# Two transformer blocks on one core: modulation transposes emitted later, four plain column blocks ahead of the quarter products

## The chip, the core and the metric

The kernel runs on one core of a Trainium2 chip. The metric is the device time of one execution in microseconds (us), lower is better. TensorE (PE) does the matrix products; its weight loads (PEld) overlap them. ScalarE (ACT), VectorE (DVE) and GpSimd (POOL) do the elementwise work, and SyncE's queue (SP) issues every DMA. An engine works through its own queue in order.

## The reference

`reference()` computes two blocks in float32 on a sequence of 1024 tokens with 1024 features. What matters here is the swiglu layer, which the first block holds twice, and the modulation that comes from a conditioning vector:

```python
def swiglu(h, w_gu, w_down):
    g, u = jnp.split(h @ w_gu, 2, axis=-1)        # w_gu: 1024 x 5632
    return (jax.nn.silu(g) * u) @ w_down          # w_down: 2816 x 1024

mod = (cs @ w_ada[l] + b_ada[l]).reshape(B, N_MOD, D)      # first block, 9 x 1024
mod = c @ w_ada[l] + b_ada[l]                              # second block, 3 x 1024, for l = 0, 1
x = x + HALF_STEP * gt1 * swiglu(h, w_gu1[l], w_down1[l])  # FFN 1; then the mixer; then FFN 2
```

## The kernel before

**Precision.** Every float32 matrix is split into a high and a low part. `split` (line 262 onwards) makes the high part with a copy on ACT (line 255) and the low part with a subtraction on DVE (line 277). One product of a 128x128 weight block with a 128x512 half of the tokens is then three matmuls: high by high, high by low, low by high (lines 328 to 330, or 601 to 603).

**The FFN.** `ffn` (line 629) runs twice, as FFN 1 (0 to 740 us of the trace) and FFN 2 (1480 to 2060 us). The 2816 columns are 22 blocks of 128, each with a gate half and an up half. The first `n` = 3 blocks are plain: `gu_start` or `gu` multiplies gate and up for one half of the tokens, 8 x 3 matmuls each, so a block takes 2 x 2 x 24 = 96 matmuls. Their weights go through the queue `ws` (class `Weights`): `get(i, ahead)` splits view i at once if that has not happened yet, and fetches and splits further views only as far as `ahead` says. The other 19 blocks go through `products` (line 558), a seven-product scheme on quarters: 7 products of 4 x 3 matmuls, 84 per block. For it `combine` (line 517) forms sums of token quarters (`hs`, `ht`, `T`) on DVE, POOL and ACT, beside the plain blocks of the second token half. For each product the weight quarters `a11` to `s4` are made by POOL sums (`ws` tiles, line 574) and split by ACT and DVE into a `W` pair; `prep` does that LAG = 4 products ahead. The two raw tiles of a block are loaded by `fetch`. Finished activations are split (`act`) and stored to DRAM by `spill`. Then the down stage (`out`) multiplies by `w_down`.

**Modulation chunks.** `ada` (line 436) makes 512 columns of a modulation vector as filler beside the products: four loads (`adaw`), eight multiply-adds on DVE into `adacc` (lines 454 and 456), then four PE transposes (line 469) and a DVE sum along the row (line 471). For the gate rows of the second block a product with ones (line 488) takes the place of the transposes. `fill()` starts a chunk: `beside(n)` calls it ahead of product n when n % 14 is 3 and n is under 105, and the down stage calls it twice per group from its second group on while chunks are left (14 chunks in FFN 1, 12 in FFN 2).

**Order.** The code emits work through `Pipe`: `go` starts a generator and steps it and all live ones, and `products` steps them once after each product. The framework's planner then makes each engine's queue out of that order: it may let a ready instruction pass one that still waits. Tiles of one tag share a fixed number of slots: 43 of 4 KB per partition (tag "u": weights, splits, `H`, `T`, `W`, `act`, loads), 14 of 2 KB (tag "hf": `ws`, `pc`, `pq`, `e`, `adacc`) and 8 PSUM banks (`ps`).

```python
pipe.until(lambda: (id(H), "combined") in self.ready)      # end of the plain blocks
...
fetch(0)                                                   # products: raw weights of its first two blocks
fetch(1)
for n in range(-1, self.LAG):
    prep(n)                                                # first sums and splits
```

Of the kernel before, what the change touches and what calls it, by code (L numbers as in the profile page):

```python
# [18 lines left out]
P = 128  # L19
T = 1024  # L20
HT = 512
NK = 8
DFF = 2816
NFF = DFF // P
# [26 lines left out]
class Pipe:  # L51
# [25 lines left out]
    def beside(self):  # L77
        for f in self.side:
            f.feed(self)
# [81 lines left out]
class Weights:  # L161
# [7 lines left out]
    def fetch(self, n):  # L169
        while len(self.stg) < min(n, len(self.views)):  # L170
            self.stg.append(self.load(*self.views[len(self.stg)]))
# [21 lines left out]
class Build:  # L193
# [239 lines left out]
                self.nc.vector.tensor_tensor(p[:, 1], t, p[:, 0].bitcast(F32), OP.subtract)  # L433
            yield

    def ada(self, w, c, bias, out, c0, row=None, ahead=False):


        nc = self.nc
        def load(q):  # L440
            t = self.U(F32, (P, 2, 512), "adaw")
            self.load(t, w[c0 // HT][:, 2 * q:2 * q + 2])
            return t

        if ahead:
            ts = [load(q) for q in range(4)]
            yield
        acc = self.half(name="adacc")
        for q in range(4):
            t = ts[q] if ahead else load(q)  # L450
            for j in range(2):
                k = 2 * q + j
                if k == 0:
                    nc.vector.tensor_scalar(acc, t[:, j], c[:, k:k + 1], None, OP.mult)
                else:
                    nc.vector.scalar_tensor_tensor(acc, t[:, j], c[:, k:k + 1], acc, OP.mult, OP.add)
            if not ahead:
                yield
        if row is not None:
            b = self.half(name="brow")  # L460
            self.load(b[0:1], row[1])
            ps = self.total(acc)
            yield
            nc.vector.scalar_tensor_tensor(b[0:1], ps[0:1], 1.0, b[0:1], OP.add, OP.add)
            self.store(row[0], b[0:1])
            return
        ps = self.ps([P, 4, P])
        for j in range(4):
            nc.tensor.transpose(ps[:, j], acc[:, j * P:(j + 1) * P], self.ident)
        f = c0 // P  # L470
        nc.vector.tensor_reduce(out[:, f:f + 4], ps, AX.X, OP.add)
        nc.vector.tensor_tensor(out[:, f:f + 4], out[:, f:f + 4], bias[:, f:f + 4], OP.add)
# [76 lines left out]
            2: ("s3", "a11", "a21", OP.subtract), 3: ("s4", "a12", "s2", OP.subtract)}  # L549
    LAG = 4  # L550

    def products(self, pairs, view, B, post, beside):

        nc, pipe = self.nc, self.pipe
        mm = nc.tensor.matmul
        seq = [(i, j) for i in range(len(pairs)) for j in range(7)]
        raw, W, Wr = {}, {}, {}

        def fetch(i):
            if i < len(pairs):
                r = [self.fetch_w(*view(pairs[i], o)) for o in range(2)]
                for o in range(2):
                    for q in range(2):
                        Wr[i, f"a{o + 1}{q + 1}"] = r[o].rearrange("p k c -> p (k c)")[:, HALVES[q]]

        def sums(n):

            for d, (name, a, b, op) in self.SUMS.items():  # L570
                if (n - d) % 7 == 0 and 0 <= (n - d) // 7 < len(pairs):
                    i = (n - d) // 7
                    Wr[i, name] = t = self.half(name="ws")
                    nc.gpsimd.tensor_tensor(t, Wr[i, a], Wr[i, b], op)

        def prep(n):
            sums(n)
            if 0 <= n < len(seq):
                i, j = seq[n]
                W[n] = p = self.pair("W")  # L580
                self.split(Wr[i, self.SEVEN[j][0]], p[:, 0], p[:, 1])
                if j == 2:
                    fetch(i + 2)

        fetch(0)
        fetch(1)
        for n in range(-1, self.LAG):
            prep(n)
        for n, (i, j) in enumerate(seq):
            beside(n)  # L590
            prep(n + self.LAG)
            if j == 0:
                acc = {s: self.ps() for s in "xyz"}
                g = post(pairs[i])
                next(g)
                started, held = set(), {}
            w, b, s = W.pop(n), B[self.SEVEN[j][1]], self.SEVEN[j][2]
            o = acc[s]
            for k in range(4):
                wh, wl = (w[:, q, k * P:(k + 1) * P] for q in range(2))  # L600
                mm(o, wh, b[k][:, 0], start=k == 0 and s not in started, stop=False, skip_group_check=True)  # L601
                mm(o, wh, b[k][:, 1], start=False, stop=False, skip_group_check=True)  # L602
                mm(o, wl, b[k][:, 0], start=False, stop=k == 3, skip_group_check=True)  # L603
            started.add(s)
            if j in (0, 2, 3):
                c = self.half(name="pc")
                self.copy(c, o)
                held[j] = c
            elif j == 6:
                g.send(o)  # L610
                pipe.start(g)
            else:
                c = self.half(name="pq")
                nc.vector.tensor_tensor(c, o, held[{1: 0, 4: 3, 5: 2}[j]], OP.add)  # L614
                g.send(c)
            pipe.step()
            pipe.beside()

    def ffn(self, H, X, XD, wgu, wdown, gate, fill, done, late, squares=True, begin=False):
# [2 lines left out]

        nc, pipe = self.nc, self.pipe

        n, kept = 3, range(18, NFF)
        groups = [[18, 19, 20]] + [list(range(f, f + 3)) for f in range(0, 15, 3)] + [[15, 16, 17, 21]]
        G = len(groups)
        act, order, views = {}, {}, []
# [13 lines left out]
        def gu(f, h, ahead=2, parts=1):  # L642
            pg, pu = self.ps(), self.ps()
            yield from self.gemm(pg, ws.get(order[f, 0], ahead), 0, H, h, parts)
            if parts > 1:
                yield
            yield from self.gemm(pu, ws.get(order[f, 1], ahead), 0, H, h, parts)
            yield
            yield from swiglu(f, h, pg, pu)
# [9 lines left out]
        def swiglu(f, h, pg, pu):  # L659
            e = self.half(name="e")  # L660
            self.act(e, pg, AF.Silu)
            nc.vector.tensor_tensor(e, e, pu, OP.mult)
            yield
            spill(f, h, e)

        def gu_start(f):
            w, p = [ws.get(order[f, o], 2 if f == o == 0 else 1) for o in range(2)], [self.ps(), self.ps()]
            for ks in range(4), range(4, NK):
                for o in range(2):
                    yield from self.gemm(p[o], w[o], 0, H, 0, 1, ks)  # L670
                yield
            yield from swiglu(f, 0, *p)
# [37 lines left out]
            ws.begin(2)  # L710
        yield
        if begin:
            items = [gu_start(f) for f in range(n)]
            for g in items:
                next(g)
            yield
            for g in items:
                pipe.go(g)
        else:
            pipe.until(self.whole(H, 0))  # L720
            for f in range(n):
                pipe.go(gu(f, 0, 2 if f == 0 else 0, 2), 4)
        pipe.until(self.whole(H, 1))
        B = {}
        sums = self.combine(H, B)
        for f in range(n):
            pipe.go(gu(f, 1, 1 if f == n - 1 else 0, 4), 8)
            if f == 0:
                pipe.start(sums)
        pipe.until(lambda: (id(H), "combined") in self.ready)  # L730
        rest = list(range(n, NFF))

        def beside(i):
            if i % 14 == 3 and i < 105:
                fill()
            if i == 7 * len(rest) - 4:
                wd.fetch(1)
            if i == 7 * len(rest) - 1:
                wd.split(1)

        self.products(rest, lambda f, o: (wgu[o * NFF + f], NK, P), B, post, beside)
        def load_x(k):
            if k < NK:
                X[k] = self.U(name="x")
# [1180 lines left out]
    def run(self):  # L1925
        nc, a, pipe = self.nc, self.a, self.pipe
        self.consts()
        cs = self.small([P, 8], name="cs")
        self.sigmoid(cs, self.v("c"))
        nc.vector.tensor_tensor(cs, cs, self.v("c"), OP.mult)  # L1930
        mod, mod2, coef = self.mod, self.mod2, self.coef
        wa = a["w_ada"]

        def ada1(c0):
            return self.ada(wa, cs, self.v("b_ada"), mod, c0, ahead=c0 < 2048)

        def ada2(l, c0):
            row = (self.g1[l][:, c0 - 2048:c0 - 1536], a["b_ada_2"][l:l + 1, c0:c0 + 512]) if c0 >= 2048 else None
            return self.ada(a["w_ada_2"][l], self.v("c_2"), self.v("b_ada_2")[:, 24 * l:24 * l + 24],
                            mod2[:, 24 * l:24 * l + 24], c0, row)  # L1940

        def scale_col(i, sc, g, ks=slice(0, 8)):
            out = coef[:, i:i + 8]
# [5 lines left out]
        H = self.new_h()  # L1949
# [71 lines left out]
        prep, rest = self.mlstm_prep(heads), Stream(second(), self.R1)  # L2021
# [29 lines left out]
        out = self.w_out(Y, YD, a["w_out"], mod[:, 40:48], X, XD, to_ffn, lambda: next(ffn))  # L2051
# [133 lines left out]
```

## Time and profile before

| | us |
|---|---|
| median of 3 runs | 3318.3 (3317.18 to 3319.18) |
| the profiled execution | 3313.98 |
| its span, first to last instruction | 3312.2 |
| PE busy in it | 3180.8 (96%) |
| DVE, ACT, POOL busy | 2218.0, 1413.6, 486.8 |

The profiled execution is 4.3 us faster than the median. Busy time of PE counts overlapping matmuls once. "Idle before" is what an engine waited ahead of an instruction, and the releaser is the work whose end let it go. The granted clock of PE is 1.00 at 2.4 GHz and 0.50 at 1.2 GHz.

### The profile page before, as it was taken

How to read it: one execution, taken by the hardware profiler on the slowest of the kernel's cores; microseconds unless marked ns; L12 is line 12 of the kernel's file. 1: busy time of each engine (PE TensorE's matmuls, PEld its weight loads, DVE VectorE, ACT ScalarE, POOL GpSimd, SP SyncE). 2: the span in 40 equal slices, each digit the busy share in tenths (PEclk: the TensorE clock that was granted, in tenths of full speed). 3: DMA queues.
4: the chain of work that ended last, by engine and by line, in shares of the span. 5: the costliest groups of instructions: out<-in, count | busy, mean ns of one | idle time of the engine just before them, and what ended most of it. 6: DMA issues, size and time to landing. Idle time of an engine off the chain costs nothing.

```text
span 3312.2 us, 38901 instructions
## 1 busy us (share of the span) xinstructions
PE 3180.8 (96%) x14420; PEld 2594.4 (78%) x14420; DVE 2218.0 (67%) x3349; ACT 1413.6 (43%) x2399; POOL 486.8 (15%) x328
## 2 busy tenths in 40 slices
PE   8799999999999979998999999999999999999998
PEld 5677788887877768886777888878888777888777
DVE  6866666746378877668666657464756886665787
ACT  4343341113466654553333421054346834444770
POOL 0533220000122243415223200000000000000000
PEclk9899999999999979999999999999999999999999
DMA  6344428714554466463444275233422333432233
GB/s 258 127 153 153 153 82 295 252 70 124 150 147 121 113 172 187 119 217 114 153 153 153 102 252 210 85 108 108 121 77 71 108 121 116 145 94 65 71 134 108
DMA packets 177261, 460.38 MB, mean 139 GB/s; under 512 B 17944, under 2 KB 20888, under 8 KB 177072
## 3 DMA queue, kind: packets, MB, share of 16 engines
q1 hardware_dynamic: 177072, 457.91, 41.9%
q8 instruction: 113, 1.85, 0.2%
q14 instruction: 76, 0.62, 0.1%
HBM read 340.19 MB, written 117.65 MB: 138 GB/s over the span
## 4 chain that ended last, share of the span: by engine, by line
PE 46%; DVE 5%; ACT 2%; issue 2%; DMA 2%; POOL 0%; SPq 0%; DVEq 0%; ACTq 0%; POOLq 0%
PE ps L328 8%; PE ps L330 8%; PE ps L329 8%; PE ps L601 2%; PE ps L603 2%; PE ps L602 2%; PE ps L1806 2%; PE ps L1882 2%; PE ps L1883 1%; PE ps L1599 1%; PE ps L1867 1%; PE ps L1600 1%; PE ps L1601 1%; PE ps L1881 1%; PE ps L1868 1%
## 5 line engine op out<-in xcount | busy, mean ns | idle before, releaser
L328 PE MATMUL ps<-H,wh 128*128 128x512 f32 x1296 | 515.7, 398 | 16.6 <-ACT wh L255 12.5
L330 PE MATMUL ps<-H,wl 128*128 128x512 f32 x1296 | 510.2, 394 | 1.9 <-DVE wl L277 1.9
L329 PE MATMUL ps<-H,wh 128*128 128x512 f32 x1296 | 508.5, 393 | 0.0
L328 PEld LDWEIGHTS ps<-H,wh 128*128 128x128 f32 x1296 | 245.9, 190 | 72.4 <-ACT wh L255 14.2
L330 PEld LDWEIGHTS ps<-H,wl 128*128 128x128 f32 x1296 | 245.7, 190 | 56.7 <-DVE wl L277 3.9
L329 PEld LDWEIGHTS ps<-H,wh 128*128 128x128 f32 x1296 | 246.2, 190 | 51.1 <-issue 1.7
L255 ACT ACTIVATE wh<-stg 128x1024 fp32r<-128x1024 f32 (+1 forms) x157 | 154.0, 990 | 308.8 <-PE ps L329 96.4
L703 DVE SCALAR_TENSOR_TENSOR x<-ps,coef,x 128x512 f32<-128x512 f32 x224 | 167.7, 750 | 165.5 <-PE ps L330 164.6
L328 PE MATMUL ps<-act,wh 128*128 128x512 f32 x704 | 276.2, 392 | 0.0
L330 PE MATMUL ps<-act,wl 128*128 128x512 f32 x704 | 274.1, 389 | 0.0
L329 PE MATMUL ps<-act,wh 128*128 128x512 f32 x704 | 273.9, 389 | 0.0
L277 DVE TENSOR_TENSOR wl<-stg,wh 128x1024 fp32r<-128x1024 f32 (+1 forms) x173 | 210.0, 1220 | 75.7 <-ACT wh L255 68.7
L601 PE MATMUL ps<-T,W 128*128 128x512 f32 x608 | 237.6, 391 | 5.5 <-DVE pq L614 4.8
L602 PE MATMUL ps<-T,W 128*128 128x512 f32 x608 | 237.3, 390 | 0.0
L603 PE MATMUL ps<-T,W 128*128 128x512 f32 x608 | 237.1, 390 | 0.0
L1809 DVE TENSOR_REDUCE bmc<-ps 128x1 f32<-128x512 f32 x256 | 164.7, 684 | 49.9 <-PE ps L1806 49.8
L601 PE MATMUL ps<-H,W 128*128 128x512 f32 x456 | 182.6, 400 | 10.7 <-ACT W L255 10.7
L250 ACT ACTIVATE bE<-ps 128x512 f32<-128x512 f32 x256 | 138.3, 590 | 102.9 <-PE ps L1868 72.6
L603 PE MATMUL ps<-H,W 128*128 128x512 f32 x456 | 179.8, 394 | 1.4 <-DVE W L277 1.4
L602 PE MATMUL ps<-H,W 128*128 128x512 f32 x456 | 179.8, 394 | 0.0
L281 DVE TENSOR_TENSOR bEl<-bE,bEh 128x1024 fp32r<-128x1024 f32 x128 | 155.3, 1218 | 33.5 <-ACT bEh L255 17.8
L614 DVE TENSOR_TENSOR pq<-ps,pc 128x512 f32<-128x512 f32 x114 | 78.5, 688 | 137.8 <-PE ps L603 137.6
(364 smaller groups left out, 7038.4 us busy)
## 6 DMA issues: line engine op xcount, KB each, us to landing
act<-act SPq DMA_DIRECT2D x144, 512.0 KB
adaw<-in_w_ada SPq DMA_DIRECT2D x120, 512.0 KB
stg<-in_w_gu SPq DMA_DIRECT2D x88, 512.0 KB
stg<-in_w_in SPq DMA_DIRECT2D x69, 512.0 KB
stg<-in_w_down SPq DMA_DIRECT2D x56, 384.0 KB
stg<-in_w_out SPq DMA_DIRECT2D x28, 512.0 KB
y<-y SPq DMA_DIRECT2D x22, 512.0 KB
x<-xspill SPq DMA_DIRECT2D x16, 512.0 KB
```

Of the source, the lines that this page charges most:

```text
L250: i = self.nc.scalar.activation(out, in_, func, **kw)
L255: self.nc.scalar.activation(out, in_, AF.Copy, scale=scale)
L277: self.nc.vector.tensor_tensor(lo, src, hi.bitcast(F32), OP.subtract)
L281: eng.tensor_tensor(lo, e, hi.bitcast(F32), OP.subtract)
L328: mm(ps, wh, rh, start=k == 0, stop=False)
L329: mm(ps, wh, rl, start=False, stop=False)
L330: mm(ps, wl, rh, start=False, stop=k == n - 1)
L601: mm(o, wh, b[k][:, 0], start=k == 0 and s not in started, stop=False, skip_group_check=True)
L602: mm(o, wh, b[k][:, 1], start=False, stop=False, skip_group_check=True)
L603: mm(o, wl, b[k][:, 0], start=False, stop=k == 3, skip_group_check=True)
L703: nc.vector.scalar_tensor_tensor(x, ps, gate[:, m:m + 1], x, OP.mult, OP.add)
L1809: nc.vector.tensor_reduce(mc[:, 8 * h + i:8 * h + i + 1], pss[h], AX.X, OP.max)
```

## The change

Four things. `ada` gets a number `late` (2 for every chunk that runs as filler): it lets two steps pass between the last multiply-add and the transposes (or the product with ones), and for the transposes two more between them and the DVE sum. `fill()` comes ahead of products with n % 14 = 8 in place of 3, which makes 7 chunks under 105 in place of 8; the remaining one moves to the down stage. The number of plain blocks `n` rises from 3 to 4, so 18 blocks are left for the products. The first half of the tokens still takes only the first three blocks at the place where it did; the fourth block runs for both halves in `ready()`, which `products` calls after its first loads, the first POOL sums and the splits of its products 0 and 1, and before the loads of its second block and the splits of products 2 and 3. The third block's `gu` call for the second half has `ahead` 0 in place of 1.

```diff
@@ -433,7 +433,7 @@
                 self.nc.vector.tensor_tensor(p[:, 1], t, p[:, 0].bitcast(F32), OP.subtract)
             yield
 
-    def ada(self, w, c, bias, out, c0, row=None, ahead=False):
+    def ada(self, w, c, bias, out, c0, row=None, ahead=False, late=0):
 
 
         nc = self.nc
@@ -459,14 +459,20 @@
         if row is not None:
             b = self.half(name="brow")
             self.load(b[0:1], row[1])
+            for _ in range(late):
+                yield
             ps = self.total(acc)
             yield
             nc.vector.scalar_tensor_tensor(b[0:1], ps[0:1], 1.0, b[0:1], OP.add, OP.add)
             self.store(row[0], b[0:1])
             return
+        for _ in range(late):
+            yield
         ps = self.ps([P, 4, P])
         for j in range(4):
             nc.tensor.transpose(ps[:, j], acc[:, j * P:(j + 1) * P], self.ident)
+        for _ in range(late):
+            yield
         f = c0 // P
         nc.vector.tensor_reduce(out[:, f:f + 4], ps, AX.X, OP.add)
         nc.vector.tensor_tensor(out[:, f:f + 4], out[:, f:f + 4], bias[:, f:f + 4], OP.add)
@@ -549,7 +555,7 @@
             2: ("s3", "a11", "a21", OP.subtract), 3: ("s4", "a12", "s2", OP.subtract)}
     LAG = 4
 
-    def products(self, pairs, view, B, post, beside):
+    def products(self, pairs, view, B, post, beside, ready):
 
 
 
@@ -583,8 +589,10 @@
                     fetch(i + 2)
 
         fetch(0)
-        fetch(1)
         for n in range(-1, self.LAG):
+            if n == 2:
+                ready()
+                fetch(1)
             prep(n)
         for n, (i, j) in enumerate(seq):
             beside(n)
@@ -622,7 +630,7 @@
 
         nc, pipe = self.nc, self.pipe
 
-        n, kept = 3, range(18, NFF)
+        n, kept = 4, range(18, NFF)
         groups = [[18, 19, 20]] + [list(range(f, f + 3)) for f in range(0, 15, 3)] + [[15, 16, 17, 21]]
         G = len(groups)
         act, order, views = {}, {}, []
@@ -710,7 +718,7 @@
             ws.begin(2)
         yield
         if begin:
-            items = [gu_start(f) for f in range(n)]
+            items = [gu_start(f) for f in range(n - 1)]
             for g in items:
                 next(g)
             yield
@@ -718,27 +726,32 @@
                 pipe.go(g)
         else:
             pipe.until(self.whole(H, 0))
-            for f in range(n):
+            for f in range(n - 1):
                 pipe.go(gu(f, 0, 2 if f == 0 else 0, 2), 4)
         pipe.until(self.whole(H, 1))
         B = {}
         sums = self.combine(H, B)
-        for f in range(n):
-            pipe.go(gu(f, 1, 1 if f == n - 1 else 0, 4), 8)
+        for f in range(n - 1):
+            pipe.go(gu(f, 1, 0, 4), 8)
             if f == 0:
                 pipe.start(sums)
-        pipe.until(lambda: (id(H), "combined") in self.ready)
+
+        def ready():
+            for h in range(2):
+                pipe.go(gu(n - 1, h, 0, 4), 8)
+            pipe.until(lambda: (id(H), "combined") in self.ready)
+
         rest = list(range(n, NFF))
 
         def beside(i):
-            if i % 14 == 3 and i < 105:
+            if i % 14 == 8 and i < 105:
                 fill()
             if i == 7 * len(rest) - 4:
                 wd.fetch(1)
             if i == 7 * len(rest) - 1:
                 wd.split(1)
 
-        self.products(rest, lambda f, o: (wgu[o * NFF + f], NK, P), B, post, beside)
+        self.products(rest, lambda f, o: (wgu[o * NFF + f], NK, P), B, post, beside, ready)
         def load_x(k):
             if k < NK:
                 X[k] = self.U(name="x")
@@ -1932,12 +1945,12 @@
         wa = a["w_ada"]
 
         def ada1(c0):
-            return self.ada(wa, cs, self.v("b_ada"), mod, c0, ahead=c0 < 2048)
+            return self.ada(wa, cs, self.v("b_ada"), mod, c0, ahead=c0 < 2048, late=2 * (c0 >= 2048))
 
         def ada2(l, c0):
             row = (self.g1[l][:, c0 - 2048:c0 - 1536], a["b_ada_2"][l:l + 1, c0:c0 + 512]) if c0 >= 2048 else None
             return self.ada(a["w_ada_2"][l], self.v("c_2"), self.v("b_ada_2")[:, 24 * l:24 * l + 24],
-                            mod2[:, 24 * l:24 * l + 24], c0, row)
+                            mod2[:, 24 * l:24 * l + 24], c0, row, late=2)
 
         def scale_col(i, sc, g, ks=slice(0, 8)):
             out = coef[:, i:i + 8]
```

## Rows read from the trace of the kernel before

**Rows 1.** The page's part 1: busy us (share of the span), instructions.
```profile
PE 3180.8 (96%) x14420; PEld 2594.4 (78%) x14420; DVE 2218.0 (67%) x3349; ACT 1413.6 (43%) x2399; POOL 486.8 (15%) x328
```

**Rows 2.** Waits of PE in FFN 1: us in total, times, longest.
```profile
PE ps L469 <- DVE adacc L456: 13.9, 8, 5.4
PE ps L601 <- ACT W L255: 8.9, 1, 8.9
...
PE ps L601 <- DVE pq L614: 1.6, 1, 1.6
```

**Rows 3.** The same of FFN 2.
```profile
PE ps L469 <- DVE adacc L456: 11.2, 6, 3.8
PE ps L601 <- DVE pq L614: 3.1, 1, 3.1
PE ps L488 <- DVE adacc L456: 2.8, 2, 1.5
PE ps L601 <- ACT W L255: 1.8, 1, 1.8
```

**Rows 4.** Timeline of PE, FFN 1: start, us, line, tiles, form, idle before, releaser.
```profile
113.66 0.39 PE L330 MATMUL ps<-H,wl 128*128 128x512 f32 x1
122.95 0.80 PE L601 MATMUL ps<-H,W 128*128 128x512 f32 x1 [8.90 <-ACT W L255]
...
131.54 0.40 PE L601 MATMUL ps<-H,W 128*128 128x512 f32 x1
131.77 0.39 PE L602 MATMUL ps<-H,W 128*128 128x512 f32 x1
...
153.97 1.11 PE L469 MATMUL ps<-ident,adacc 128*128 128x128 f32 x4 [5.37 <-DVE adacc L456]
...
158.59 0.39 PE L601 MATMUL ps<-H,W 128*128 128x512 f32 x1
```

**Rows 5.** One stretch: us, then PE, PEld, DVE, ACT, POOL busy, PEclk, DMA share, GB/s.
```profile
126.00:128.00 2.00, 2.00 (x6) 1.55 (x5) 0.00 (x0) 0.06 (x1) 1.92 (x3) 0.50 1.02 414
```

**Rows 6.** Timeline of PE, FFN 2.
```profile
1545.17 0.50 PE L601 MATMUL ps<-H,W 128*128 128x512 f32 x1 [1.83 <-ACT W L255]
...
1575.57 1.11 PE L469 MATMUL ps<-ident,adacc 128*128 128x128 f32 x4 [3.77 <-DVE adacc L456]
...
1578.50 0.40 PE L603 MATMUL ps<-H,W 128*128 128x512 f32 x1
```

**Rows 7.** Timelines of SP, ACT, DVE and POOL ahead of FFN 1's products.
```profile
117.75 3.73 SPq L285 DMA_DIRECT2D stg<-in_w_gu  x6
...
122.27 1.15 ACT L255 ACTIVATE W<-stg 128x512 fp32r<-128x512 f32 x2 [1.54 <-DMA stg<-in_w_gu]
...
117.19 7.03 DVE L277 TENSOR_TENSOR T<-ht,T 128x512 fp32r<-128x512 f32 x8
124.15 1.28 DVE L277 TENSOR_TENSOR W<-stg,W 128x512 fp32r<-128x512 f32 x2
...
124.27 2.29 POOL L574 TENSOR_TENSOR ws<-stg 128x512 f32<-128x512 f32 x1 [4.21 <-DMA stg<-in_w_gu]
```

**Rows 8.** The same of FFN 2: SP, POOL.
```profile
1539.37 4.75 SPq L285 DMA_DIRECT2D stg<-in_w_gu  x6
...
1546.69 1.55 POOL L574 TENSOR_TENSOR ws<-stg 128x512 f32<-128x512 f32 x1 [4.96 <-DMA stg<-in_w_gu]
```

**Rows 9.** Timelines of ACT and DVE: a plain block's weight split.
```profile
1497.16 1.05 ACT L255 ACTIVATE wh<-stg 128x1024 fp32r<-128x1024 f32 x1
...
1500.44 1.22 DVE L277 TENSOR_TENSOR wl<-stg,wh 128x1024 fp32r<-128x1024 f32 x1
```

**Rows 10.** Timeline of PE: the second token half of x comes in.
```profile
53.46 1.03 PE L392 MATMUL ps<-ident,xin 128*128 128x128 f32 x8
```

**Rows 11.** Two stretches (columns as in group 5): FFN 1's down stage, the mixer.
```profile
560.00:740.00 180.00, 180.00 (x804) 148.71 (x803) 115.74 (x166) 23.18 (x29) 0.00 (x0) 1.00 0.50 172
740.00:1480.00 740.00, 698.05 (x3378) 577.66 (x3377) 519.34 (x920) 401.48 (x714) 186.76 (x124) 0.97 0.51 150
```

## The prediction

> **What bounds the kernel now.** I read the page's first part before anything else: PE is busy for 3180.8 of 3312.2 us [rows 1], so time can only be won where PE waits or runs slowly, and every matmul added is paid in full. Next come the waits of PE, taken for each FFN by itself, since the change touches nothing else by hand. In FFN 1 PE waits 13.9 us ahead of the modulation transposes for the last multiply-add (eight waits, the longest 5.4), 8.9 us once for the first split of a quarter weight, and 1.6 us for a DVE sum [rows 2]. In FFN 2 the same places cost 11.2 us (six waits, the longest 3.8), 2.8 us where a product with ones takes the transposes' place, 1.8 and 3.1 us [rows 3]. The timeline of PE shows where the big ones stand: 8.90 us between the last plain matmul and the first product, and 5.37 us ahead of the first transposes [rows 4]; 1.83 and 3.77 us in FFN 2 [rows 6].
>
> The timeline shows a second loss behind the long waits. At full speed one matmul starts 0.23 us after the other (131.54 to 131.77). From 122.95 to 131.54 there are 18 of them in 8.59 us, where 18 x 0.23 = 4.1 would do [rows 4]; the granted clock in that stretch is 0.50, the 1.2 GHz level [rows 5]. So 4.4 us are lost there (a wait of 0.7 for the low part is in it). From 153.97 to 158.59 there are nine matmuls and four transposes of a quarter of the columns, ten matmul times or 2.3 us, in 4.62 us: 2.3 lost [rows 4]. In FFN 2, five matmuls and four transposes take 1575.57 to 1578.50, 2.93 us for six times 0.23: 1.6 lost [rows 6]. The short waits of 1.2 to 1.5 us I count without such a loss.
>
> **Transposes two products later.** A chunk's last multiply-add comes out at most 5.4 us after PE has reached its transposes [rows 2, 4], usually about 8.5 / 7 = 1.2. Two products are 24 matmuls of 0.23, 5.5 us, so every one of these waits is covered: by PE's own products, whose splits are made four ahead. The number of transposes does not change. The DVE sum of a row then waits for transposes that ended two products before, so nothing queued behind it on DVE is held. Removed: 13.9 - 5.4 = 8.5 us in FFN 1, 11.2 - 3.8 = 7.4 and 2.8 in FFN 2, together 18.7 us; the two first waits (5.4 and 3.8) are counted with the starts below. If the cover were gone the price would be these same waits. `adacc` keeps its hf slot and `ps` its bank longer; by the code at most eight of the 14 hf tiles are in use around a chunk, so I take nothing for it.
>
> **Fill at product 8 and one chunk moved.** The first chunk no longer falls among the late first splits. The eighth goes to the down stage, where PE has no idle at all beside six such chunks (180.00 of 180.00 us, DVE at 115.74) [rows 11]: nothing, bounded by one wait of 1.2 us per FFN.
>
> **The fourth plain block.** It replaces 84 matmuls by 96 in each FFN: 24 x 0.23 = 5.5 us added for certain.
>
> **What the starts lose now and then.** Removed in FFN 1: 8.9 + 4.4 + 1.6 (a DVE sum stuck behind the chunk's multiply-adds) + 5.4 + 2.3 = 22.6 us [rows 2, 4]. In FFN 2: 1.8 + 3.1 + 3.8 + 1.6 = 10.3 us [rows 3, 6]. The 22 us that the fourth block gives PE to do (96 x 0.23) run beside the sums of token quarters, the first POOL sums and the first four splits.
>
> But the fourth block needs weights, and here the change adds waits. Views 6 and 7 are its gate and up weights. In FFN 1 they are loaded with the early ones, and view 6 is split early too. View 7 is split only when `gu` gets to its up half, behind the splits of products 0 and 1 and the third block's activation. PE ends the third block at 114.05 and has the gate half, 24 x 0.23 = 5.5 us, so it wants view 7 at 119.6. ACT is held until 122.27, since SP issues the quarter weights' loads only at 117.75, behind an activation store [rows 7]. Two W splits (1.15), an activation split (half of that) and the high part (1.05) [rows 7, 9] put view 7 at 125.0: PE waits 5.5. DVE ends those W parts at 124.15 + 1.28, then 0.6 and 1.22 for the low part [rows 7, 9]: 127.3, where the third matmul could have begun at 125.5: 1.8 more. After a wait of 5.4 us the clock cost 2.3, so 9.6 us in all. Queued behind that matmul on PE are the block's second token half and all products.
>
> In FFN 2 neither view is prefetched: with `ahead` 0 view 6 is loaded when it is to be split. Its load stands third on SP, behind the two that start at 1539.37; the second of them lets POOL go at 1546.69 [rows 8]. One load lands 2.0 us after the other in FFN 1 (122.27 and 124.27, rows of ACT and POOL) [rows 7], so view 6 is there at 1548.7 and its high part at 1549.7. PE ended the third block at 1545.17 - 1.83 = 1543.3 [rows 6]: it waits 6.4, for the low part 0.8 more, and 2.3 for the clock: 9.5 us. View 7's load is next on SP and its split is ready well within the gate half. Together 19.1 us of new losses. The lower bound is none, if the planner gets these splits ahead of the others. The upper bound is that the starts lose the 32.9 us of before.
>
> The Trainium skill has a rule against this place. "SBUF — State Buffer", section "Who interferes with whom", says that a VectorE instruction with two SBUF inputs competes with a GpSimd instruction that reads SBUF, and that one of them blocks until the other is through. The trace agrees as far as it goes: eight T subtractions beside POOL take 7.03 us, 0.88 each, two W ones 1.28, 0.64 each [rows 7]. By that rule the low parts of views 6 and 7 could each wait for one more POOL sum; at the 1.55 us of rows 8 the sum below would be 3.1 us higher, 3294.3.
>
> The loads of the products' second block now follow the fourth block and its stores on SP. They are wanted at product 3, behind the second token half (48 x 0.23 = 11 us) and three products (8 us), and take about 5 us to land (117.75 to 122.27) [rows 7]: nothing. In FFN 1's first token half two more loads (1 MB, 2.5 us at the 414 GB/s of rows 5) and one split come ahead of the second half of x. Its transposes follow PE's other work without a wait [rows 10], so I take nothing; without that cover it would be up to 2.5 us.
>
> **Sum.** Removed 22.6 + 10.3 + 18.7 = 51.6; added 5.5 + 19.1 = 24.6; net 27.0 us less. The profiled execution (3313.98 us, span 3312.2) would come to 3287.0. It lies 4.3 us under the median of 3318.3, from which the forecast is made: 3291.3 us.
>
> **Rivals.** *No new waits.* The splits of views 6 and 7 come in time; then only the matmuls are added: 51.6 - 5.5 = 46.1 less, 3272.2 us. For it speaks that view 7's raw tile is long there in FFN 1, against it the order of the tiles and SP's late issue. *The starts gain nothing.* Beside the fourth block the 43 slots of tag u are nearly full (16 H, 16 T, four weight parts, two raw tiles, two W, one or two activations by the code), so the next raw tiles and W pairs wait for PE to free some, and what the starts lost comes back as other waits. Then 18.7 - 5.5 = 13.2 less, 3305.1 us. *The change doesn't do what it says.* The planner orders the queues by its own model; if it places the transposes right behind their sums again, 13.9 + 11.2 + 2.8 us of waits and the 3.9 us of slow clock stay: 27.0 - 31.8, or 4.8 us more, 3323.1. Against it: PE follows the code's order closely in this trace, and the transposes are now written two products later. *Slower.* The planner sorts the queues of the later stages anew, since its clock has shifted. The place is the mixer, where PE idles 740.00 - 698.05 = 42 us [rows 11]. If its waits doubled, the sum would be 42 - 27 = 15 us more, 3333.3; it decides from 27 us of added idle on. Nothing in the code of that stage changes, so it is unlikely.
>
> **How the numbers follow.** The forecast (3280 to 3300 by the bounds of the new waits) gets 0.55, no new waits 0.14, starts without gain 0.17, the unmoved transposes 0.08, the mixer 0.06. The range reaches from a little below the first rival to a little above the second: 3268 to 3308, with 0.86 inside. A measurement can tell about 0.2%, 6.6 us, from no change. Faster by more: the first three, 0.86; within: 0.08; slower: 0.06.
>
> **What would show it.** In the changed kernel's waits of PE, the rows "L469 <- adacc" and "L488 <- adacc" should be gone. Ahead of the products no wait for W should stand, and PE should wait 5 to 7 us inside the fourth block, for wh of view 7 in FFN 1 and for the load and wh of view 6 in FFN 2, followed by a stretch at clock 0.50. Matmuls of lines 328 to 330 should be 64 more per line and those of 601 to 603 56 fewer. The down stages should still show no idle. I am wrong if waits for adacc remain, if products stop for W or pq after the fourth block, or if idle outside the FFNs changes by more than a few us.

## The result and the profile after

| | before | after |
|---|---|---|
| median, us | 3317.7 (4 runs) | 3287.2 (4 runs) |
| ratio to before, 95% interval | | 0.9909 [0.9892, 0.9926] |
| span of the profiled execution, us | 3312.2 | 3285.2 |

The change makes the kernel 0.9% faster, 30.5 us by the medians. The forecast was 3291.3 us with a range of 3268 to 3308. In the profiled executions the span is 27.0 us shorter. Times are medians of fast executions; one of the four of e4_fill3 took 15802.6 us at a granted clock of 0.186 and is left out.

The page's first part after the change (rows 1 before): PE's busy time falls by 3.2 us although 24 matmuls were added, and its idle time from 131.4 to 107.6 us. A matmul at the slow clock counts as busy for longer, so what is won in slow stretches stands in the busy time.

```profile
PE 3177.6 (97%) x14444; PEld 2596.1 (79%) x14444; DVE 2214.4 (67%) x3333; ACT 1406.1 (43%) x2383; POOL 460.5 (14%) x320
```

The waits of PE up to 740 us, FFN 1 (rows 2 before; us in total, times, longest). `wh` and `wl` are the high and low part of a plain block's weights. No line for adacc is left, and none for W. Of the 14.6 us for wh, 10.4 are new; the other 4.2 us stood at the first matmul of the kernel before too.

```profile
PE ps L328 <- ACT wh L255: 14.6, 2, 10.4
...
PE ps L330 <- DVE wl L277: 1.4, 2, 0.7
...
PE ps L609 <- DVE pq L622: 0.8, 2, 0.6
```

The same for FFN 2, 1480 to 2060 us (rows 3 before; FFN 2 now begins at 1459.00, and PE waits nowhere between there and 1480). Here too everything about adacc has gone, and 4.0 us for wh and 4.0 us for wl stand in its place.

```profile
PE ps L330 <- DVE wl L277: 5.0, 2, 4.0
PE ps L328 <- ACT wh L255: 4.6, 2, 4.0
PE ps L609 <- DVE pq L622: 0.6, 2, 0.3
```

The timeline of PE in FFN 1 (rows 4 before). The fourth block starts behind the third without a gap; after its gate half PE stops for 10.41 us. From 130.94 to 139.16 there are 17 matmuls in 8.22 us, at a granted clock of 0.50 from 131 to 138; at 0.23 each they would take 3.9.

```profile
120.14 0.39 PE L330 MATMUL ps<-H,wl 128*128 128x512 f32 x1
130.94 0.79 PE L328 MATMUL ps<-H,wh 128*128 128x512 f32 x1 [10.41 <-ACT wh L255]
...
132.78 0.79 PE L330 MATMUL ps<-H,wl 128*128 128x512 f32 x1 [0.61 <-DVE wl L277]
...
139.16 0.40 PE L330 MATMUL ps<-H,wl 128*128 128x512 f32 x1
```

In FFN 2 (rows 6 before) PE stops ahead of the first matmul of the fourth block and again two matmuls later. Between 1537 and 1541 the granted clock is 0.50; at 1541.92 PE is back at full pace.

```profile
1531.51 0.77 PE L328 MATMUL ps<-H,wh 128*128 128x512 f32 x1 [4.03 <-ACT wh L255]
1532.07 0.63 PE L329 MATMUL ps<-H,wh 128*128 128x512 f32 x1
1536.71 0.79 PE L330 MATMUL ps<-H,wl 128*128 128x512 f32 x1 [4.01 <-DVE wl L277]
...
1541.92 0.40 PE L330 MATMUL ps<-H,wl 128*128 128x512 f32 x1
```

Where the 27 us went is read from the first matmul of three stages: FFN 1's down stage, FFN 2's first plain block, FFN 2's down stage. Before:

```profile
512.64 0.39 PE L328 MATMUL ps<-act,wh 128*128 128x512 f32 x1
...
1474.91 0.39 PE L328 MATMUL ps<-H,wh 128*128 128x512 f32 x1
...
1936.15 0.39 PE L328 MATMUL ps<-act,wh 128*128 128x512 f32 x1
```

After:

```profile
499.18 0.39 PE L328 MATMUL ps<-act,wh 128*128 128x512 f32 x1
...
1459.00 0.39 PE L328 MATMUL ps<-H,wh 128*128 128x512 f32 x1
...
1908.54 0.39 PE L328 MATMUL ps<-act,wh 128*128 128x512 f32 x1
```

FFN 1 up to its down stage is 13.5 us shorter (512.64 to 499.18). FFN 2 up to its down stage took 461.2 us and takes 449.5, 11.7 less. What lies between, with the mixer, went from 962.3 to 959.8, and the rest from 1376.1 to 1376.7.

### The profile page after: what moved, and what is told of

It is laid out like the page before. It is cut to its first block, busy times and chain, and to the rows that moved or that the text cites. A ratio compares the mean times of both kernels' runs of the same rounds, so it can differ in the third digit from the quotient of the medians.

```text
span 3285.2 us, 38924 instructions
## 1 busy us (share of the span) xinstructions
PE 3177.6 (97%) x14444; PEld 2596.1 (79%) x14444; DVE 2214.4 (67%) x3333; ACT 1406.1 (43%) x2383; POOL 460.5 (14%) x320
## 4 chain that ended last, share of the span: by engine, by line
PE 50%; DVE 3%; ACT 2%; issue 1%; DMA 1%; DVEq 0%; ACTq 0%
PE ps L328 8%; PE ps L330 8%; PE ps L329 8%; PE ps L609 3%; PE ps L611 3%; PE ps L610 3%; PE ps L1613 2%; PE ps L1612 2%; PE ps L1614 2%; PE ps L1819 2%; PE ps L1895 1%; PE ps L1896 1%; PE ps L1894 1%; PE ps L1880 1%; PE ps L1881 1%
## 5 line engine op out<-in xcount | busy, mean ns | idle before, releaser
L328 PE MATMUL ps<-H,wh 128*128 128x512 f32 x1360 | 542.9, 400 | 30.9 <-ACT wh L255 27.1
L330 PE MATMUL ps<-H,wl 128*128 128x512 f32 x1360 | 536.9, 395 | 6.8 <-DVE wl L277 6.7
L329 PE MATMUL ps<-H,wh 128*128 128x512 f32 x1360 | 534.9, 393 | 0.0
L328 PEld LDWEIGHTS ps<-H,wh 128*128 128x128 f32 x1360 | 259.1, 191 | 90.4 <-ACT wh L255 29.6
L330 PEld LDWEIGHTS ps<-H,wl 128*128 128x128 f32 x1360 | 258.4, 190 | 66.2 <-DVE wl L277 10.6
L329 PEld LDWEIGHTS ps<-H,wh 128*128 128x128 f32 x1360 | 259.3, 191 | 53.8 <-issue 1.7
L609 PE MATMUL ps<-T,W 128*128 128x512 f32 x576 | 224.6, 390 | 1.4 <-DVE pq L622 1.4
L611 PE MATMUL ps<-T,W 128*128 128x512 f32 x576 | 224.2, 389 | 0.0
L610 PE MATMUL ps<-T,W 128*128 128x512 f32 x576 | 224.1, 389 | 0.0
L609 PE MATMUL ps<-H,W 128*128 128x512 f32 x432 | 170.1, 394 | 0.0
L611 PE MATMUL ps<-H,W 128*128 128x512 f32 x432 | 168.2, 389 | 0.0
L610 PE MATMUL ps<-H,W 128*128 128x512 f32 x432 | 168.1, 389 | 0.0
```

The source lines that it names most:

```text
L328: mm(ps, wh, rh, start=k == 0, stop=False)
L329: mm(ps, wh, rl, start=False, stop=False)
L330: mm(ps, wl, rh, start=False, stop=k == n - 1)
```

## The experiments

Nine kernels. Every ratio is to runs of the kernel before on the same chip; the medians of the kernel before lay between 3314.7 and 3317.7 us. The columns FFN 1 and FFN 2 are the two stretches just described, in the profiled execution (512.6 and 461.2 before).

| kernel | us | ratio, 95% interval | FFN 1 | FFN 2 |
|---|---|---|---|---|
| changed kernel | 3287.2 | 0.9909 [0.9892, 0.9926] | 499.2 | 449.5 |
| e1_late_only | 3280.4 | 0.9899 [0.9886, 0.9911] | 497.3 | 445.6 |
| e2_no_late | 3303.1 | 0.9968 [0.9956, 0.9980] | 503.9 | 457.1 |
| e3_early_views | 3261.3 | 0.9841 [0.9828, 0.9853] | 483.6 | 437.9 |
| e4_fill3 | 3283.7 | 0.9907 [0.9892, 0.9921] | 495.4 | 448.0 |
| e5_late_fill8 | 3272.8 | 0.9866 [0.9851, 0.9881] | 491.9 | 440.0 |
| e6_fetch_only | 3285.5 | 0.9908 [0.9894, 0.9923] | 496.3 | 449.7 |
| e7_views_late1 | 3275.7 | 0.9873 [0.9856, 0.9889] | 488.7 | 443.7 |
| e8_half_deferred | 3282.5 | 0.9897 [0.9882, 0.9912] | 492.7 | 442.9 |
| e9_ready_first | 3279.8 | 0.9900 [0.9884, 0.9917] | 493.6 | 446.2 |

### e1_late_only: the delays alone

The edit, to the kernel before (the row form and the two calls get `late` as in the change); fill, `n` and `products` stay as they are there.

```diff
-    def ada(self, w, c, bias, out, c0, row=None, ahead=False):
+    def ada(self, w, c, bias, out, c0, row=None, ahead=False, late=0):
...
+        for _ in range(late):
+            yield
         ps = self.ps([P, 4, P])
         for j in range(4):
             nc.tensor.transpose(ps[:, j], acc[:, j * P:(j + 1) * P], self.ident)
+        for _ in range(late):
+            yield
```

> The kernel before with the two delays of `late` alone: chunks still start at n % 14 = 3, three plain blocks, first splits where they were. Theory A (the forecast's terms add up, the block is worth what its sum says): the steady waits of 8.5 + 7.4 + 2.8 us go, and the two first waits (5.4, 3.8) with 3.9 us of slow clock too, since the transposes come 5.5 us later and the last multiply-add was at most 5.4 late: 31.8 us less, about 3286 us, and the start of the products still shows 8.9 us (FFN 1) and 1.8 us (FFN 2) of waits for W. By this the rest of the change is worth about nothing. Theory B (the late multiply-adds are a lack of VectorE throughput, so the wait only moves to another DVE product): the waits for adacc go but waits for pq or W of 1 us a chunk take their place, 0 to 9 us less, 3309 to 3318 us.

Measured: 3280.4 us, 0.9899. That is as fast as the whole change (the intervals overlap) and somewhat faster than theory A's 3286. The waits of PE in FFN 1 show no adacc, while the old wait ahead of the products stands as before:

```profile
PE ps L607 <- ACT W L255: 8.8, 1, 8.8
...
PE ps L607 <- DVE pq L620: 2.1, 1, 2.1
PE ps L609 <- DVE W L277: 1.9, 1, 1.9
```

FFN 1 is 15.3 us shorter than before and FFN 2 15.7. Theory B falls: no wait takes the place of the 14 steady ones. What followed from the forecast's own terms also holds: the rest of the change, as placed, brings nothing on top of the delays.

### e2_no_late: the change without the delays

```diff
-            return self.ada(wa, cs, self.v("b_ada"), mod, c0, ahead=c0 < 2048, late=2 * (c0 >= 2048))
+            return self.ada(wa, cs, self.v("b_ada"), mod, c0, ahead=c0 < 2048, late=0)
...
-                            mod2[:, 24 * l:24 * l + 24], c0, row, late=2)
+                            mod2[:, 24 * l:24 * l + 24], c0, row, late=0)
```

> The changed kernel with late = 0: fourth plain block, early splits and fill at n % 14 = 8 stay. Theory A: about 14 waits for adacc of 1.2 to 1.5 us are back, 18.7 us, none of them over 2 us since the first chunk is clear of the late splits: 3305 to 3307 us. Theory B (block and fill carry the gain, the delays none): within 4 us of the changed kernel's 3287.

Measured: 3303.1 us, 0.9968. The waits of PE in FFN 1, and below them those of FFN 2:

```profile
PE ps L473 <- DVE adacc L456: 7.4, 7, 1.4
```

```profile
PE ps L473 <- DVE adacc L456: 4.9, 5, 1.4
...
PE ps L494 <- DVE adacc L456: 2.8, 2, 1.5
```

These 15.1 us over 14 chunks, none longer than 1.5, are back, and the time with them: 15.9 us more than the changed kernel by the medians, 0.0059 or 19.6 us by the ratios. Theory A holds in kind, though the time is 2 us under the 3305 to 3307 that it expected; the delays are worth what the steady waits cost, 18.7 us by the forecast.

### e3_early_views: the fourth block's weights earlier

```diff
         for f in range(n - 1):
+            if f == 1:
+                ws.fetch(2 * n)
+            if f == 2:
+                ws.split(2 * n)
             pipe.go(gu(f, 1, 0, 4), 8)
```

> The changed kernel with the fourth block's weights brought forward: all eight views fetched before the second block's second-half call, all split before the third's. Theory A (PE's waits inside the fourth block, 10.4 + 0.6 us in FFN 1 and 4.0 + 4.0 us in FFN 2, with some 4 us of slow clock behind each, come only from where these splits and loads stand): they go, and nothing takes their place: 22 to 28 us less than the changed kernel, 3259 to 3265 us. Theory C (the 43 slots of tag u are full there, so T pairs and raw quarter tiles get their slots later by as much as the views get theirs earlier): the waits move to the first products, gain under 8 us, 3279 to 3287 us.

Measured: 3261.3 us, 0.9841, the fastest of all, 26 us under the changed kernel. All that is left of waits in FFN 1 once the second token half has begun is

```profile
PE ps L609 <- ACT pc L255: 1.0, 2, 0.5
PE ps L609 <- DVE pq L622: 0.2, 1, 0.2
```

and in FFN 2 nothing behind its first block. FFN 1 is 15.6 us shorter than in the changed kernel, FFN 2 11.6. Theory A holds and theory C falls: the slots suffice. So the waits inside the fourth block, with the slow clock behind them, came from where the splits and loads of its weights stood in the queues.

### e4_fill3: chunks at the old place

```diff
-            if i % 14 == 8 and i < 105:
+            if i % 14 == 3 and i < 105:
```

> The changed kernel with chunks started at n % 14 = 3 again (8 in the products, 6 or 4 in the down stage). Theory A (W pairs are four ahead when the products start, so the first chunk finds room at product 3 too): within 3 us of the changed kernel, 3284 to 3290. Theory D (the burst of multiply-adds at products 3 to 5 holds the DVE sum pq of product 4, for which product 6 waits): the waits of 1.6 and 3.1 us for pq are back with the slow clock behind them, 5 to 9 us more, 3292 to 3296.

Measured: 3283.7 us, 0.9907 against 0.9909: no difference that shows, as theory A had it (it allowed 3 us; the medians are 3.5 apart). Theory D falls: no wait for pq comes back in either FFN.

### e5_late_fill8: delays and new chunk place, without the fourth block

The kernel of e1_late_only with

```diff
-            if i % 14 == 3 and i < 105:
+            if i % 14 == 8 and i < 105:
```

> The kernel before with the delays and with chunks at n % 14 = 8; three plain blocks, no deferred block. In e1_late_only (3280.4 us) PE still waited 2.1 us in FFN 1 and 2.7 us in FFN 2 for pq with 2 us of slow clock behind each. Theory A (the first chunk's multiply-adds hold that DVE sum): these go, 7 to 9 us less than e1, 3271 to 3274 us. Theory E (the sum is late because the W pairs are still catching up after the late start): they stay, 3278 to 3282 us.

Measured: 3272.8 us, 0.9866, by the medians 7.6 us under e1 and inside theory A's 3271 to 3274. The waits for pq of 2.1 and 2.7 us are gone. Where products start late, the place of the first chunk does count. Together with e1 this prices the rest of the change: the fourth block and the early splits, as placed, take the kernel from 0.9866 to 0.9909, some 14 us more.

### e6_fetch_only: the loads earlier, the splits not

```diff
         for f in range(n - 1):
+            if f == 1:
+                ws.fetch(2 * n)
             pipe.go(gu(f, 1, 0, 4), 8)
```

> The changed kernel with all eight views fetched early, but split where it splits them. FFN 1 is the changed kernel's, since its views were loaded early there already. Theory A (the order of the splits on ACT and DVE is what PE waits for in the fourth block, as in FFN 1): in FFN 2 only the 0.9 us that ACT waited for the load goes, and the wait for the low part of view 6, 4.0 us, stays: 3284 to 3287 us. Theory F (the missing prefetch is the cause in FFN 2): its 8.0 us of waits and some 3 us of slow clock go, 3275 to 3278 us.

Measured: 3285.5 us, 0.9908, the changed kernel's time, as theory A had it. In FFN 2 the wait for wh falls to 2.6 us and that for wl grows to 5.9:

```profile
PE ps L330 <- DVE wl L277: 6.9, 2, 5.9
PE ps L328 <- ACT wh L255: 3.1, 2, 2.6
```

So the missing prefetch, on which the forecast laid the waits in FFN 2, is not enough to explain them: with the loads early PE reaches the low part earlier and waits longer there, 8.5 us in place of 8.0 in all. What holds the low part is taken up under e9.

### e7_views_late1: one product of delay

The kernel of e3_early_views with `late` 1 in place of 2 in both calls:

```diff
-            return self.ada(wa, cs, self.v("b_ada"), mod, c0, ahead=c0 < 2048, late=2 * (c0 >= 2048))
+            return self.ada(wa, cs, self.v("b_ada"), mod, c0, ahead=c0 < 2048, late=1 * (c0 >= 2048))
...
-                            mod2[:, 24 * l:24 * l + 24], c0, row, late=2)
+                            mod2[:, 24 * l:24 * l + 24], c0, row, late=1)
```

> e3_early_views (3261.3 us) with late = 1 in place of 2. Theory A (PE has to be covered for 1.2 to 1.5 us per chunk, and one product is 2.7 us): the same within 3 us, no waits for adacc. Theory G (the multiply-adds are pushed back by what PE does meanwhile, so the wait follows the transposes): waits for adacc of up to 1 us come back at most of the 14 chunks, 5 to 14 us more.

Measured: 3275.7 us, 0.9873, 14 us over e3. The waits of PE in FFN 1, and below them those of FFN 2:

```profile
PE ps L473 <- DVE adacc L456: 2.9, 6, 0.8
```

```profile
PE ps L473 <- DVE adacc L456: 3.0, 5, 0.9
PE ps L494 <- DVE adacc L456: 2.0, 2, 1.3
```

Theory A falls, and so does theory G's reason, although its numbers nearly fit. The multiply-adds were not pushed back, but the transposes moved by less than a product. The stretches run from a chunk's first multiply-add to its transposes; the number in brackets counts the products' matmuls that PE ran in them. First e2 (no delay), then e7 (one), then e3 (two):

```profile
251.02:264.19 13.17, 12.41 (x55) 1.00 0.82 274
238.67:252.50 13.83, 13.09 (x58) 1.00 0.78 261
236.49:252.13 15.64, 15.64 (x70) 1.00 0.68 231
```

The chunk's last multiply-add starts 11.9, 12.5 and 12.2 us after its first, so it stays where it was. The first step of delay is worth 3 matmuls (0.7 us), the second 12 (2.7 us): without a delay the planner had already put nine matmuls of a product ahead of the transposes, in each of these 14 chunks. The waits of 0.8 to 1.5 us less these 0.7 come near what e7 shows, 0.1 to 1.3. Of the 14 us, 7.9 are these waits. The mixer is some 3 us longer (720.9 against 718.1 us from its first product to FFN 2). The remaining 3 are within the spread of the runs.

### e8_half_deferred: three plain blocks, half of the third deferred

The changed kernel with

```diff
-        n, kept = 4, range(18, NFF)
+        n, kept = 3, range(18, NFF)
...
-            items = [gu_start(f) for f in range(n - 1)]
+            items = [gu_start(f) for f in range(n)]
...
-            for f in range(n - 1):
+            for f in range(n):
                 pipe.go(gu(f, 0, 2 if f == 0 else 0, 2), 4)
...
-            for h in range(2):
-                pipe.go(gu(n - 1, h, 0, 4), 8)
+            pipe.go(gu(n - 1, 1, 0, 4), 8)
```

> The changed kernel with three plain blocks, of which only the third's second token half runs in ready(), behind the first quarter splits: 24 matmuls fewer, no views 6 and 7. Theory A (what the start needs is the first splits early and 11 us of plain work beside them; products 0 and 1 read no T): the 5.5 us of added matmuls go and the waits ahead of the products are 4 us or less in each FFN: 3254 to 3264 us. Theory H (the fourth block's 22 us are needed, since the last T pairs come later still with the POOL sums and W splits put ahead of them): PE waits 5 to 10 us at product 2 for T in each FFN and slows down behind it: 3268 to 3285 us.

Measured: 3282.5 us, 0.9897: theory H. In FFN 1 PE stops at the first product that reads T, and again two matmuls on. The timelines of PE, and below it of ACT ahead of that:

```profile
127.27 0.79 PE L609 MATMUL ps<-T,W 128*128 128x512 f32 x1 [9.72 <-ACT pc L255]
...
131.18 0.79 PE L611 MATMUL ps<-T,W 128*128 128x512 f32 x1 [2.69 <-DVE W L277]
```

```profile
122.69 0.63 ACT L255 ACTIVATE T<-ht 128x512 fp32r<-128x512 f32 x1 [5.38 <-POOL ht L539]
123.91 1.15 ACT L255 ACTIVATE T<-ht 128x512 fp32r<-128x512 f32 x2 [0.59 <-POOL ht L539]
...
126.64 0.58 ACT L255 ACTIVATE pc<-ps 128x512 f32<-128x512 f32 x1
```

The copy pc that lets PE go stands on ACT behind the splits of the token sums T, and ACT stands there for POOL's sums. In FFN 2 PE waits 2.3 and 3.2 us at the same products, less than the 5 to 10 of theory H. With the quarter weights early and less plain work ahead, the token sums are what is late. Even so FFN 1 and FFN 2 are 6.5 and 6.7 us shorter than in the changed kernel; the stretch between them is 7.5 us longer and hides most of it in the total. The fourth block's 22 us thus have a use, and its 5.5 us of added matmuls buy something once its own weights don't come late (e3 against e5: 0.9841 to 0.9866).

### e9_ready_first: no splits ahead of the fourth block

```diff
         fetch(0)
+        ready()
+        fetch(1)
         for n in range(-1, self.LAG):
-            if n == 2:
-                ready()
-                fetch(1)
             prep(n)
```

> The changed kernel without the splits ahead: the first raw loads, then the fourth block, then the second raw loads and all of prep. Theory A (in the fourth block PE waits for weight parts that stand behind the W splits and the POOL sums beside them): the W subtractions, 3.4 us in each FFN, and in FFN 1 the two W copies no longer stand ahead: 3 to 4 us less wait in each FFN, and the W pairs are still ready after 22 us of plain work: 3277 to 3282 us. Theory I (the splits ahead are what keeps PE going at the first products): waits for W of 3 us or more appear ahead of product 0 in both FFNs and the time is 3287 to 3297 us.

Measured: 3279.8 us, 0.9900, inside theory A. By the medians this is 7.4 us under the changed kernel, by the ratios 3, with intervals that overlap; the FFNs of the profiled execution are 5.6 and 3.3 us shorter. The timeline of DVE in FFN 1 shows the two W subtractions gone from ahead of the third block's activation:

```profile
117.26 7.07 DVE L277 TENSOR_TENSOR T<-ht,T 128x512 fp32r<-128x512 f32 x8
124.25 0.67 DVE L669 TENSOR_TENSOR e<-e,ps 128x512 f32<-128x512 f32 x1
```

The longest wait for wh is 7.1 us in place of 10.4 (that for wl behind it 1.6 in place of 0.6), and no product waits for W. In FFN 2 the wait for view 6's low part falls from 4.0 us to 0.6, while the one for its high part stays, 4.2 us. The splits ahead of the fourth block are thus no gain: they stand in the way of its own weights, and 22 us of plain work are enough to make them behind it.

## Why the prediction was right

**Transposes later: right in kind and size.** All waits for adacc are gone, in both FFNs and in both forms. Priced at 18.7 us; e2 gives 15.9 by the medians and 19.6 by the ratios. What the forecast didn't see is that the cover was smaller than the two products' 24 matmuls, 5.5 us, that it counted: against e2 the transposes stand 15 matmuls later, 3.4 us. That is still more than the 1.5 us of the longest steady wait; one product would not have been enough (e7).

**The added matmuls: right.** The matmuls of lines 328 to 330 that read `H` rise by 64 each (1296 to 1360), those of the products' three lines fall by 56 each (1064 to 1008).

**Waits inside the fourth block: foreseen, in the right places, and too small.** In FFN 1 the forecast had 9.6 us, 7.3 of waiting (of it 5.5 at view 7, where it allowed 5 to 7) and 2.3 of slow clock. Measured are 10.4 and 4.3 us (8.22 less 3.9, a wait of 0.6 in it), 14.7 in all: 3.7 more of waiting, 1.4 more of slow clock. The step that failed is the order on DVE: the price took the third block's activation to be done in passing, at 0.6 us on ACT. The timelines of ACT and of DVE show the chain:

```profile
123.40 1.15 ACT L255 ACTIVATE W<-stg 128x512 fp32r<-128x512 f32 x2 [1.55 <-DMA stg<-in_w_gu]
...
129.31 0.63 ACT L255 ACTIVATE act<-e 128x512 fp32r<-128x512 f32 x1 [4.27 <-DVE e L670]
129.85 1.04 ACT L255 ACTIVATE wh<-stg 128x1024 fp32r<-128x1024 f32 x1
```

```profile
118.27 7.07 DVE L277 TENSOR_TENSOR T<-ht,T 128x512 fp32r<-128x512 f32 x8
125.27 3.41 DVE L277 TENSOR_TENSOR W<-stg,W 128x512 fp32r<-128x512 f32 x2
128.60 0.67 DVE L670 TENSOR_TENSOR e<-e,ps 128x512 f32<-128x512 f32 x1
```

View 7's copy stands behind the activation's copy on ACT (129.31), that one waits for a DVE product (128.60), and that one for two W subtractions that took 3.41 us in place of the 1.28 of rows 7. So PE's wait runs T, W, e, act, wh, all on these two engines. e9 takes the W part out and the wait falls by 3.3 us; e3 takes the whole chain out and the wait is gone.

In FFN 2 the forecast had 9.5 us, measured are 4.0 and 7.2 (10.41 us from 1531.51 to 1541.92 for 14 matmuls of 0.23, the second wait in it), 11.2. The forecast saw one cause there, the late load of view 6, and 0.8 us for the low part. The timelines of ACT and of DVE show two:

```profile
1527.83 1.15 ACT L255 ACTIVATE W<-stg 128x512 fp32r<-128x512 f32 x2 [1.29 <-DMA stg<-in_w_gu]
...
1530.39 1.06 ACT L255 ACTIVATE wh<-stg 128x1024 fp32r<-128x1024 f32 x1 [0.92 <-DMA stg<-in_w_gu]
```

```profile
1531.02 3.42 DVE L277 TENSOR_TENSOR W<-stg,W 128x512 fp32r<-128x512 f32 x2
1534.37 0.68 DVE L670 TENSOR_TENSOR e<-e,ps 128x512 f32<-128x512 f32 x1
1534.97 1.69 DVE L277 TENSOR_TENSOR wl<-stg,wh 128x1024 fp32r<-128x1024 f32 x1
```

The first 4.0 us end with view 6's copy, which stands on ACT behind the W copies and then 0.9 us for its load. The second 4.0 us end with its low part, which stands on DVE behind the W subtractions. Loads earlier alone (e6) turn 4.0 and 4.0 us into 2.6 and 5.9; the W splits out of the way alone (e9) turn them into 4.2 and 0.6; with both parts of the weights made early (e3) both are gone.

**The sum: right by terms that partly cancel.** In the profiled executions the forecast and the result are both 27.0 us, and that they agree so closely is luck. (By the medians 30.5 us were won: the profiled execution of the changed kernel lies at its median, not 4.3 us under it as the one before did.) By stage they differ. FFN 1: forecast 31.1 removed and 12.3 added (half of the matmuls), 18.8 less; measured 13.5 less, since the new wait is 5.1 us longer than priced. FFN 2: forecast 20.5 removed and 12.3 added, 8.2 less; measured 11.7 less. The new waits there are 1.7 us longer than priced, and yet more was won: the sum left out the slow matmuls behind the wait of 3.1 us (twelve that start from 1567.19 to 1571.28, 1.6 us over their pace) and the small waits for the copy pc and the low part of W at the first products, 0.7 and 0.6 us. These are 2.9 of the 5.2 us; where the others went stays open. Elsewhere 1.8 us, below what these profiles can assign.

**The rivals.** *No new waits* was not the changed kernel, but it is e3: priced at 3272.2 us, measured 3261.3; 5.5 of these 11 us are won in FFN 2 (23.3 us against 17.8 by the sum), as in the changed kernel. *The starts gain nothing* comes out 18 us too high; the starts of the changed kernel do lose 25.9 of the 32.9 us that they won, but to the order of splits and loads and not to slots, since e3 holds two more split tiles earlier and loses nothing. *The unmoved transposes* fall: no wait for adacc is left. *The mixer*: from its first product to the start of FFN 2 (755.76 to 1474.91 us before; FFN 1's down stage runs past 740), where nothing was edited by hand, the ten changed kernels take 716 to 724 us and the kernel before 719; that is the size of what the planner's new sorting does, far from the 27 us at which it would have decided.

**The rule about VectorE and GpSimd.** "SBUF — State Buffer", section "Who interferes with whom" of the Trainium skill, had a stronger say than the forecast gave it, which put 3.1 us beside its sum (3291.3 and 3.1 make 3294.4, not 3294.3). The Trainium skill adds there that the order of issue decides which of the two waits. The traces agree: before, the W subtractions began at 124.15, ahead of POOL's sum at 124.27, and took 1.28 us for two while the sum took 2.29 [rows 7], where the next two sums, begun while DVE was idle, took 1.27 and 1.28. After, POOL began first, at 125.02, and the two subtractions took 3.41:

```profile
125.02 1.44 POOL L580 TENSOR_TENSOR ws<-stg 128x512 f32<-128x512 f32 x1 [3.84 <-DMA stg<-in_w_gu]
126.54 1.59 POOL L580 TENSOR_TENSOR ws<-ws,stg 128x512 f32<-128x512 f32 x1
```

## What to carry to other kernels

Where PE waits for the last step of a filler, move the consumer and not the filler, and count in the trace how far it moved: here one product in the code was 3 matmuls in PE's queue and left half of the waits, two left none. Work that is put ahead as cover needs its own inputs made earlier still; a split that is written at the point of use stands behind everything queued before it on both engines that make it. And price the parts apart: the delays alone brought 33 us, the cover as placed cost some 14 beside the same kernel without it, and with its weights made ready earlier the whole change gained 26 us more.

## What the runs showed of the hardware

**VectorE beside GpSimd.** A tensor subtraction on DVE that ran 0.64 us took 1.7 us behind a POOL sum that had begun 0.25 us earlier; a start earlier by 0.12 us put the cost on POOL. In these two traces the engine that started later was the one that paid.

**TensorE's clock.** In FFN 2 of the changed kernel two waits of 4.0 us with two matmuls between them left PE at the 1.2 GHz level, with starts 0.43 us apart up to 1541.57. The waits of 1.0 to 1.5 us at the chunks of the kernel before were each followed by a granted clock of 1.00. In between the length of the wait does not settle it: the wait of 1.8 us in rows 6 did not slow PE, while one of 1.7 us at the same place in e1 was followed by 0.71 over 5 us. Early in FFN 1 all eleven kernels have the same wait of 1.90 us for `H`. In eight of them the 5 us behind it show 0.66 to 0.70, in e2, e4 and e8 1.00. The kernel before, then e2, with PE's matmuls in the first brackets:

```profile
62.31:67.31 5.00, 5.00 (x15) 3.99 (x16) 4.25 (x11) 2.07 (x3) 0.00 (x0) 0.66 0.75 297
62.46:67.46 5.00, 5.00 (x22) 3.89 (x22) 4.24 (x11) 2.07 (x3) 0.00 (x0) 1.00 0.75 297
```

Seven matmuls fewer are 1.6 us, so a difference of that size between two of these kernels need not come from the edit.
